# A table of 39 moves in the list scheduler of a hybrid encoder layer

## The chip, the core and the metric

The kernel runs on one core of a Trainium2 chip. The metric is the device time of one execution in microseconds. Five engines work at once, each strictly in the order of its own instruction queue: TensorE (PE, the matmuls), VectorE (DVE), ScalarE (ACT), GpSimd (POOL), and SyncE (SP), which does nothing here but issue DMAs. An instruction that has to wait for a semaphore holds up everything behind it on its engine, and a DMA that has to wait holds up every later DMA of the kernel, since all of them are issued from SP.

## The reference

One layer of a streaming encoder runs over 2048 prompt positions and, with its own state, over 32 positions of a second sequence (2080 columns together). All values are fp32. Cut to what matters:

```python
cs  = silu(c); mod = cs @ ada_w + ada_b                  # six vectors: shift, scale, gate, twice
h   = rmsnorm(x, g1) * (1 + sc1) + sh1
p   = h @ w_in                                           # 1024 -> 3080 columns
u, v = split(gelu(p[:, :1024])); v = rmsnorm(v)
a   = u * (W_s @ v + b_s)                                # spatial gating in chunks of 128 positions
q, k, v2 = split(silu(causal_conv(p[:, 1024:2560])))     # 4 heads of 128; q, k L2-normed
b   = gated_delta_rule(q, k, v2, beta, g, state)         # exact, evaluated in chunks (WY form)
b   = rmsnorm(b) * silu(z)
x   = x + gt1 * (concat(a, b) @ w_out)
h   = rmsnorm(x, g2) * (1 + sc2) + sh2
x   = x + gt2 * (relu(h @ w_up)**2 @ w_down)             # 1024 -> 4096 -> 1024
y   = rmsnorm(x, g3)
```

## The kernel before

**Tiling.** The activations lie transposed, channels on the 128 partitions, positions along the free dimension. The positions are worked in two halves (1024 and 1056 columns), and a half in groups of 512, or of 384, 384 and 288 columns. Every fp32 operand of a large product is split into a rounded part and a remainder (`BH` and `BL` for activations, `wh` and `wl` for weights), and a product is three matmuls, high by high, low by high and high by low, in `mm3`. A tile of the input projection is eight such triples (k = 0 to 7), accumulated in one PSUM bank. Three banks in a ring, called `g`, hold these tiles, so a tile can begin only when the tile three before it has been copied out by ACT. The feed-forward part runs over three blocks of positions with a Strassen form of the products; its PSUM tiles are called `f`.

**Stages.** First the adaLN modulation and the z columns, then for each half: the v columns and the spatial gating, the q, k, v columns with convolution (`qkv_tile`), for each head the local part of the delta rule (`delta_local`, PSUM bank `L`) and the inversion of its triangular blocks (`delta_inv`, bank `B`), the recurrence over the chunks (`delta_chain`, bank `C`), and the u columns. Then the output projection and the feed-forward part.

**Where the steps of the prediction stand.** `x_stats` runs in the middle of half 0 and prepares half 1. For each of the three groups of columns of half 1 it loads the eight 128-row pieces of x (`s<-xT`), squares them on ACT, adds the squares on POOL, turns the sums into 1/rms on PE (bank `M`, tile `M<-ones`) and writes normalised pieces back to DRAM (`h_d<-s`); the pieces pass through a ring of four half tiles named `E` (slots 21 and 22). `load_group` later loads these `h_d` pieces as the input of half 1, through the same ring. `qkv_tile` copies a PSUM tile out on ACT (`s<-g`), convolves on DVE (`L393`), applies SiLU on ACT, transposes 32 by 32 blocks on DVE (`L419`), writes q and k to DRAM (`kq_d<-s`) and the transposed blocks too (`kt_d<-s`). `delta_local` loads a pair of chunks of k and q back (`s<-kq_d`) and multiplies them on PE into bank `L`. Weights arrive by `wr<-w_b` and are split by ACT (`wh`) and DVE (`wl`).

**What sets the order.** The kernel records every operation as an `Op` with an engine, a class (`CHAIN`, `INV`, `LOCAL`, `EVAC`, `GEMM`), an estimated cost and its predecessors, 14596 operations in all. `Program.schedule` then replays them as a list scheduler: it keeps a modelled clock for each engine, lets an operation become ready when its predecessors' modelled ends and latencies have passed, and on each engine takes the ready operation with the smallest key. The key is the class, then a rank (for `EVAC` and `GEMM` the earliest matmul that depends on the operation, for the others its number), then the number. The order of the modelled starts is the order in which the instructions are emitted, and it fixes each engine's queue. Helpers record each operation, so that most instructions of a kind share one line: matmuls L436, transposes through PE L447, activations L373, DVE and POOL two-operand instructions L388 and L393, DMAs L426.

Of the kernel before, what the change touches and what calls it, by code (L numbers as in the profile page):

```python
# [45 lines left out]
PE, DVE, ACT, POOL, DMA, NONE = range(6)  # L46
# [15 lines left out]


CHAIN, INV, LOCAL, EVAC, GEMM, IDLE = range(6)
SLACK = 400
CALM = 1500
HOLD = {CHAIN: 300, INV: 300, LOCAL: 2000}
# [147 lines left out]
class Program:  # L215
# [19 lines left out]
    def op(self, eng, cost, fn, outs, ins, lat=0.0, table=None, after=()):  # L235
# [12 lines left out]
        o.hold = HOLD.get(self.prio, 0.0) if self.lax else 0.0  # L248
        o.slack = (SLACK if self.prio < GEMM else 0.0) + self.calm if eng == PE else 0.0
        o.npred, o.due = len(preds), self.due  # L250
# [5 lines left out]
    def schedule(self):  # L256

        ops = self.ops
        due = [i if o.eng == PE and o.prio == GEMM else len(ops) for i, o in enumerate(ops)]
        for i in reversed(range(len(ops))):  # L260
            due[i] = min([due[i]] + [due[j] for j in ops[i].succ] + ([] if ops[i].due is None else [ops[i].due]))
        turn = {LOCAL: EVAC, EVAC: LOCAL}
        key = [(o.prio if o.eng == PE else turn.get(o.prio, o.prio), due[i] if o.prio >= EVAC else i, i) for i, o in enumerate(ops)]
        free = [0.0] * 6
        port = [0.0] * 6
        wait = [[] for _ in range(6)]
        ready = [([], []) for _ in range(6)]
        table, large = None, True
        order, served, lands, flying = [], 0.0, [], []

        def release(i, t):
            o = ops[i]
            if o.eng == NONE:
                finish(i, t, t)
            else:
                heapq.heappush(wait[o.eng], (t, i))

        def finish(i, start, end):
            o = ops[i]
            o.start = start  # L280
            order.append((start, i))
            for j in o.succ:
                s = ops[j]
                s.ready = max(s.ready, end + o.lat + LATENCY.get((o.eng, s.eng), 0.0) + (s.slack if o.eng != PE else 0.0))
                s.npred -= 1
                if s.npred == 0:
                    release(j, s.ready)

        for i, o in enumerate(ops):
            if o.npred == 0 and o.start == 0.0 and o.eng != NONE:  # L290
                heapq.heappush(wait[o.eng], (0.0, i))
        for i, o in enumerate(ops):
            if o.npred == 0 and o.eng == NONE and not any(k == i for _, k in order[-1:]):
                finish(i, 0.0, 0.0)
                o.npred = -1

        other = {DVE: POOL, POOL: DVE}
        while True:
            best = None
            for e in range(5):  # L300
                shared = port[other[e]] - PORT if e in other else 0.0
                t = None
                if ready[e][0]:
                    t = free[e]
                elif ready[e][1]:
                    t = max(free[e], shared)
                if wait[e]:
                    at, i = wait[e][0]
                    at = max(free[e], at, shared if ops[i].port else 0.0)
                    t = at if t is None else min(t, at)  # L310
                if t is not None and (best is None or t < best[0]):
                    best = (t, e)
            if best is None:
                break
            t, e = best
            while wait[e] and wait[e][0][0] <= t:
                i = heapq.heappop(wait[e])[1]
                heapq.heappush(ready[e][ops[i].port if e != PE else ops[i].prio == GEMM], key[i])
            shared = port[other[e]] - PORT if e in other else 0.0
            tops = [q for q in (ready[e][0], ready[e][1] if shared <= t else None) if q]  # L320
            if not tops:
                continue
            top = min(tops, key=lambda q: q[0])
            if e == PE and large and len(tops) == 2 and all(t < ops[q[-1]].ready + ops[q[-1]].hold for q in tops[0]):
                top = tops[1]
            i = heapq.heappop(top)[-1]
            o = ops[i]
            end = t + o.cost
            if e == DMA and t < EARLY:
                t = max([t] + lands[-8:-7])  # L330
                flying = [q for q in flying if q[0] > t]
                over = sum(q[1] for q in flying) + o.runs - RUNS
                if over > 0:
                    for at, q in flying:
                        over -= q
                        if over <= 0:
                            break
                    heapq.heappush(wait[e], (at, i))
                    continue
                served = max(served, t + 2330) + o.size / (310 if t < 30000 else 350) + 50  # L340
                lands.append(served)
                flying.append((served, o.runs))
                end, o.lat = t + o.turn, served - t - o.turn + (0 if t < 30000 else 1000)
            if e == PE:
                large = o.prio == GEMM
            elif o.table and o.table != table:
                end += 1280
                table = o.table
            free[e] = end
            if o.port:  # L350
                port[e] = end
            finish(i, t, end)
        assert len(order) == len(ops), (len(order), len(ops))
        self.span = max(free)
        order.sort()
        return [ops[i] for _, i in order]
# [1747 lines left out]
```

## Time and profile before

| | |
|---|---|
| median of 3 runs | 2298.68 us (2298.04 to 2300.31) |
| the profiled execution's own time | 2300.34 us |
| its span, first to last instruction | 2298.2 us |
| PE busy | 2266.2 us (99%) |
| DVE, ACT, POOL busy | 1684.5, 1201.3, 554.0 us (73%, 52%, 24%) |
| DMA engines busy, mean | 73.1% of the span on the queue that SP issues to |

An engine's busy time is the union of its instructions; the ends of matmuls are modelled, since they are pipelined, so the distance between the starts of two matmuls says more than the length of one. PE is the bound where it is busy; where it is idle, the view of waits names what it waited for. The granted clock of TensorE is listed by stretch: 1.00 is full speed.

### The profile page before, as it was taken

To read this page: it belongs to the slowest core of one execution; us is meant where nothing else is said; L and a number is where in the kernel's file an instruction comes from. 1 tells how busy PE (TensorE), PEld (TensorE's weight loads), DVE (VectorE), ACT (ScalarE), POOL (GpSimd) and SP (SyncE) were. 2 spreads that over 40 slices of the span, in tenths; PEclk is the share of its full clock that TensorE was granted. 3 is DMA by queue.
4 is the path that set the end of the run, shared out by engine and by line. 5 is a ranking of instruction groups with operands and counts; after the bars stand their busy time and mean duration, and the time that the engine had idled before them with its cause. 6 is when DMAs were issued, how large, how long until landed. Compare 5 with 4: busy or idle time off the path is not lost.

```text
span 2298.2 us, 44733 instructions
## 1 busy us (share of the span) xinstructions
PE 2266.2 (99%) x15711; PEld 2155.6 (94%) x15711; DVE 1684.5 (73%) x3560; ACT 1201.3 (52%) x2556; POOL 554.0 (24%) x708
## 2 busy tenths in 40 slices
PE   9999899999999999999999999999999999999998
PEld 6787678999999889999999999999999999999998
DVE  7557676678763646599999989776668885666775
ACT  5555455665543534476555546653444564344344
POOL 1114431322313032444444424200001250000001
PEclk9999999999999999999999999999999999999999
DMA  9588877567666767987777777997668797666761
GB/s 331 166 277 262 225 206 227 164 183 188 155 174 195 250 198 238 298 281 259 256 253 264 251 271 249 342 312 234 213 214 267 253 309 231 218 219 216 248 220 55
DMA packets 426209, 538.49 MB, mean 234 GB/s; under 512 B 132976, under 2 KB 259324, under 8 KB 425984
## 3 DMA queue, kind: packets, MB, share of 16 engines
q1 hardware_dynamic: 425984, 535.63, 73.1%
q8 instruction: 124, 2.03, 0.4%
q14 instruction: 101, 0.83, 0.1%
HBM read 386.30 MB, written 149.18 MB: 233 GB/s over the span
## 4 chain that ended last, share of the span: by engine, by line
PE 85%; DMA 5%; DVE 4%; ACT 2%; SPq 2%; issue 1%; POOL 1%; POOLq 0%; DVEq 0%; ACTq 0%
PE f L436 53%; PE g L436 24%; PE C L436 3%; PE B L436 2%; SPq L426 2%; DVE s L393 2%; ACT s L373 1%; DVE s L388 1%; PE M L436 1%; PE L L436 1%; DMA s<-kq_d 1%; DMA s<-xT 1%; DVE wl L388 1%; DMA wr<-w_b 0%; DMA s<-x_d 0%
## 5 line engine op out<-in xcount | busy, mean ns | idle before, releaser
L373 ACT ACTIVATE s<-s 128x348 f32<-128x348 f32 (+13 forms) x1083 | 506.9, 492 | 327.0 <-DVE s L388 140.3
L436 PE MATMUL f<-s,wh 128*128 128x348 f32 (+1 forms) x2768 | 662.1, 322 | 0.4 <-DVE s L388 0.4
L436 PEld LDWEIGHTS f<-s,wh 128*128 128x128 f32 x2768 | 480.5, 188 | 2.0 <-DVE s L388 1.5
L388 DVE TENSOR_TENSOR s<-f,s 128x348 f32<-128x348 f32 (+1 forms) x696 | 348.1, 512 | 170.6 <-PE f L436 166.9
L436 PE MATMUL f<-s,wl 128*128 128x348 f32 (+1 forms) x1384 | 444.8, 321 | 0.1
L436 PE MATMUL g<-BH,wh 128*128 128x384 f32 (+2 forms) x1104 | 405.8, 368 | 0.9 <-ACT BH L373 0.8
L436 PE MATMUL g<-BL,wh 128*128 128x384 f32 (+2 forms) x1104 | 388.2, 352 | 0.5 <-DVE BL L393 0.5
L436 PE MATMUL g<-BH,wl 128*128 128x384 f32 (+2 forms) x1104 | 387.9, 351 | 0.4 <-DVE wl L388 0.4
L388 DVE TENSOR_TENSOR s<-s,s 128x348 fp32r<-128x348 f32 (+9 forms) x651 | 345.6, 560 | 45.1 <-ACT s L373 20.2
L436 PE MATMUL f<-BH,wh 128*128 128x348 f32 (+1 forms) x1024 | 330.0, 322 | 0.5 <-DVE s L388 0.5
L436 PE MATMUL f<-BL,wh 128*128 128x348 f32 (+1 forms) x1024 | 329.2, 321 | 0.0
L436 PE MATMUL f<-BH,wl 128*128 128x348 f32 (+1 forms) x1024 | 328.7, 321 | 0.0
L388 POOL TENSOR_TENSOR s<-s,s 128x512 f32<-128x512 f32 (+17 forms) x303 | 237.5, 788 | 369.2 <-ACT s L373 165.8
L373 ACT ACTIVATE wh<-s 128x512 fp32r<-128x512 f32 x282 | 176.4, 632 | 233.4 <-PE f L436 189.1
L436 PEld LDWEIGHTS f<-s,wl 128*128 128x128 f32 x1384 | 260.5, 188 | 0.4 <-DVE wl L388 0.4
L388 DVE TENSOR_TENSOR wl<-s,wh 128x512 fp32r<-128x512 f32 x282 | 217.4, 778 | 33.1 <-ACT wh L373 30.4
L436 PEld LDWEIGHTS g<-BH,wh 128*128 128x128 f32 x1104 | 208.5, 189 | 24.7 <-issue 5.6
L436 PEld LDWEIGHTS g<-BH,wl 128*128 128x128 f32 x1104 | 208.0, 188 | 20.2 <-DVE wl L388 0.8
L436 PEld LDWEIGHTS g<-BL,wh 128*128 128x128 f32 x1104 | 208.2, 189 | 17.1 <-DVE BL L393 0.8
L373 ACT ACTIVATE wh<-wr 128x512 fp32r<-128x512 f32 (+2 forms) x159 | 124.2, 782 | 134.7 <-PE f L436 60.8
L436 PEld LDWEIGHTS f<-BH,wh 128*128 128x128 f32 x1024 | 192.4, 188 | 1.1 <-DVE s L388 0.8
L436 PEld LDWEIGHTS f<-BH,wl 128*128 128x128 f32 x1024 | 193.0, 189 | 0.0
(129 smaller groups left out, 3133.1 us busy)
## 6 DMA issues: line engine op xcount, KB each, us to landing
s<-w_u SPq DMA_DIRECT2D x124, 256.0 KB, 3.6
s<-w_d SPq DMA_DIRECT2D x121, 256.0 KB, 3.2
wh<-su_d SPq DMA_DIRECT2D x114, 256.0 KB, 3.9
wl<-su_d SPq DMA_DIRECT2D x114, 256.0 KB, 4.1
wh<-sd_d SPq DMA_DIRECT2D x100, 256.0 KB, 3.2
wl<-sd_d SPq DMA_DIRECT2D x100, 256.0 KB, 3.7
wr<-w_b SPq DMA_DIRECT2D x36, 512.0 KB, 5.0
s<-adaw SPq DMA_DIRECT2D x32, 512.0 KB, 7.0
```

The costliest lines, as they stand in the source:

```text
L373: self.p.op(ACT, c, lambda: nc.scalar.activation(out=R(out), in_=R(in_), func=func, **{k: R(v) for k, v in kw.items()}), [out, accum], [in ...
L388: self.p.op(eng, c, lambda: e.tensor_tensor(out=R(out), in0=R(a), in1=R(b), op=op), [out], [a, b])
L393: self.p.op(DVE, c, lambda: nc.vector.scalar_tensor_tensor(out=R(out), in0=R(a), scalar=R(s), in1=R(b), op0=op0, op1=op1), [out], [a, s, b])
L426: self.p.op(DMA, max(500, x), lambda: nc.sync.dma_start(out=R(out), in_=R(in_)), [out], [in_], lat=LAND + b / RATE - max(500, x))
L436: nc.tensor.matmul(R(out), R(l), R(r), **kw)
```

## The change

The scheduler takes a table `MOVES` of 39 rows `(first, n, shift, ns)`. A row applies to those of the n operations from number `first` on that have the engine and the class of operation `first`. `shift` is added to their rank in the key; `ns` is added to the time at which they become ready in the scheduler's modelled clock (nothing in the emitted program waits for it). No operation is added, removed or altered, and the tiles stay in the same places; only the order of the instructions on the engines changes, and with it the points at which one engine waits for another. 30 rows have a delay, 9 a shift.

```diff
+MOVES = [
+    (1137, 6, 0, 785), (4449, 24, 0, 1), (35, 1, -6283, 0), (6079, 1, 0, 13035), (195, 40, 0, 156), (1608, 40, 0, 3551),
...
+]
...
-        key = [(o.prio if o.eng == PE else turn.get(o.prio, o.prio), due[i] if o.prio >= EVAC else i, i) for i, o in enumerate(ops)]
+        rank = [due[i] if o.prio >= EVAC else i for i, o in enumerate(ops)]
+        late = [0.0] * len(ops)
+        for first, n, shift, ns in MOVES:
+            for j in range(first, min(first + n, len(ops))):
+                if (ops[j].eng, ops[j].prio) == (ops[first].eng, ops[first].prio):
+                    rank[j] += shift
+                    late[j] += ns
+        key = [(o.prio if o.eng == PE else turn.get(o.prio, o.prio), rank[i], i) for i, o in enumerate(ops)]
...
                 if s.npred == 0:
+                    s.ready += late[j]
                     release(j, s.ready)
```

The orders differ in the two halves of the mixer (the first 900 us of the profile before) and in patches of the first block of the feed-forward part up to about 1495 us. Behind that no instruction changes its place. The source has 18 more lines, so L436 before is L454 after, L426 is L444, L373 is L391. The numbers in the tiles' names count emitted tiles and differ for the same tile; g_3019 before and g_2964 after are the same tile of the input projection, and so are g_2890 and g_2866, and g_2742 and g_2755.

PE in half 0, where head 2's `delta_local` begins: bank `L` multiplies the first loaded pair of chunks, and `M<-ones` sums the squares of the third group of `x_stats`. Before:

```order
L436 MATMUL g_2890<-BH_78,wh 128x512
L436 MATMUL g_2890<-BL_86,wh 128x512
L436 MATMUL g_2890<-BH_78,wl 128x512
L436 MATMUL L_2894<-s_474 128x256 x2
L436 MATMUL M_2643<-ones,s_478 128x1 x3
L436 MATMUL g_3019<-BH_71,wh 128x512
L436 MATMUL g_3019<-BL_79,wh 128x512
```

After (the rows of g_2964 that stand ahead of these are its first three triples, BH_71 to BH_73, behind the last one of g_2866):

```order
L454 MATMUL g_2964<-BH_74,wh 128x512
L454 MATMUL g_2964<-BL_82,wh 128x512
L454 MATMUL g_2964<-BH_74,wl 128x512
L454 MATMUL L_2858<-s_474 128x256 x2
L454 MATMUL g_2964<-BH_75,wh 128x512
L454 MATMUL g_2964<-BL_83,wh 128x512
L454 MATMUL g_2964<-BH_75,wl 128x512
```

Four triples of the next tile now stand ahead of the `L` pair, and the `M` sums, which stood right behind it, stand twenty triples later.

SP's queue ahead of the load that this `L` pair multiplies (`s_474<-kq_d_99`, two DMAs). Before:

```order
L426 DMA nd_d_0_163<-s_491 16x8x16 x8
L426 DMA s_489<-xT 128x288 x2
L426 DMA kt_d_0_105<-s_475 32x32x32
L426 DMA s_488<-xT 128x288
L426 DMA kq_d_99<-s_487 128x512
L426 DMA s_488<-xT 128x288
L426 DMA s_473<-nd_d_0_163 128x256
L426 DMA kq_d_99<-s_487 128x512
L426 DMA wr_96<-w_b 128x1024
L426 DMA pk_d_3_126<-s_473 128x256
L426 DMA s_489<-xT 128x288
L426 DMA s_474<-kq_d_99 128x2x256 x2
```

After:

```order
L444 DMA pk_d_3_126<-s_473 128x256
L444 DMA nd_d_0_163<-s_491 16x8x16 x8
L444 DMA h_d_159<-s_489 128x384
L444 DMA h_d_160<-s_489 128x384
L444 DMA h_d_161<-s_488 128x384
L444 DMA h_d_162<-s_488 128x384
L444 DMA kq_d_99<-s_487 128x512 x2
L444 DMA s_473<-nd_d_0_163 128x256
L444 DMA s_489<-xT 128x288 x2
L444 DMA s_488<-xT 128x288 x2
L444 DMA s_474<-kq_d_99 128x2x256 x2
L444 DMA wr_96<-w_b 128x1024
```

Of all DMAs ahead of the load, from the start of the kernel, six are behind it now: five loads of x for the third group and one of weights; none has come ahead of it. The last `kt_d` write, which stood between the loads of x, stands ahead of the eight `nd_d` writes now, and the four `h_d` writes of the second group have come down to this place.

ACT at the same place: copies of PSUM tiles (`s_485<-g_...`), squares of the third group (128x288), SiLU and squares of the convolved tiles (`s_487`, `s_486`). Before:

```order
L373 ACTIVATE s_478<-s_489 128x288
L373 ACTIVATE s_489<-s_489 128x288
L373 ACTIVATE s_488<-s_488 128x288 x2
L373 ACTIVATE wh<-wr_96 128x1024
L373 ACTIVATE s_489<-s_489 128x288 x2
L373 ACTIVATE s_488<-s_488 128x288
L373 ACTIVATE s_486<-s_475 128x512
L373 ACTIVATE s_488<-s_488 128x288
L373 ACTIVATE s_486<-s_475 128x512
L373 ACTIVATE s_486<-s_485,s_484 128x512 x2
L373 ACTIVATE wh<-wr_96 128x1024
L373 ACTIVATE s_485<-g_2742 128x512
```

After:

```order
L391 ACTIVATE s_486<-s_475 128x512 x2
L391 ACTIVATE s_486<-s_485,s_484 128x512 x2
L391 ACTIVATE wh<-wr_96 128x1024
L391 ACTIVATE s_485<-g_2755 128x512
L391 ACTIVATE s_485<-g_2848 128x512
L391 ACTIVATE s_487<-s_486 128x512 x2
L391 ACTIVATE s_478<-s_489 128x288
L391 ACTIVATE s_489<-s_489 128x288
```

The eight squares of the third group stood ahead of the copy of the tile (g_2742, now g_2755); they all stand behind it and behind the next tile's copy now.

6 rows, old and new, of the table MOVES are left out of this document.

## The prediction

> **What bounds the kernel now.** I read the totals first, then the windows by stage, then the view of PE's waits, and last the timelines around the longest one.
>
> ```profile
> span 2298.2 us, 44733 instructions
> ```
>
> The windows give, for each stretch, its length and the busy time of PE, PEld, DVE, ACT and POOL, then the granted clock of TensorE:
>
> ```profile
> core 0: us, PE busy (x) PEld busy (x) DVE busy (x) ACT busy (x) POOL busy (x), PEclk, DMA share, GB/s
> 0.00:200.00 200.00, 195.20 (x1308) 151.97 (x1308) 126.02 (x287) 110.57 (x199) 41.86 (x62) 1.00 0.77 258
> 200.00:277.64 77.64, 77.57 (x346) 63.09 (x344) 55.77 (x103) 39.38 (x76) 31.65 (x39) 1.00 0.86 235
> 277.64:281.90 4.26, 0.00 (x1) 0.00 (x0) 2.01 (x3) 2.13 (x5) 2.47 (x6) 0.99 0.89 290
> 281.90:286.10 4.20, 0.00 (x0) 0.02 (x1) 4.09 (x7) 2.29 (x3) 3.81 (x7) 0.50 0.94 324
> 286.10:292.10 6.00, 5.99 (x17) 5.05 (x18) 3.51 (x6) 2.13 (x5) 3.40 (x8) 0.50 0.38 104
> 292.10:370.00 77.90, 77.90 (x774) 63.38 (x774) 55.25 (x108) 41.27 (x75) 21.86 (x40) 1.00 0.78 216
> 370.00:780.00 410.00, 402.30 (x3891) 388.22 (x3890) 281.53 (x827) 233.67 (x581) 103.50 (x275) 1.00 0.66 185
> 780.00:1500.00 720.00, 718.10 (x4403) 695.66 (x4402) 591.73 (x1080) 408.70 (x863) 280.12 (x213) 1.00 0.78 264
> 1500.00:2277.00 777.00, 777.00 (x4908) 776.90 (x4907) 551.57 (x1121) 353.03 (x736) 61.25 (x58) 1.00 0.72 232
> 2277.00:2298.20 21.20, 12.13 (x77) 11.28 (x75) 13.04 (x25) 8.10 (x16) 4.11 (x4) 0.78 0.38 134
> ```
>
> PE is the bound everywhere, and a change of order adds and removes no matmul. What it can win is PE's idle time, length minus busy time of a row: 4.8 us in the first 200, 8.5 between 277.64 and 286.10, nothing up to 370, 7.7 up to 780, 1.9 up to 1500, nothing up to 2277, 9.1 in the tail. To this comes a clock of 0.50 from 281.9 on, the only dip before the tail. From about 1495 on no instruction changes its place, so the tail's 9.1 us stay. About 23 us stand in stretches that the table touches, and half of that is one event.
>
> **The event.** The waits of PE (engine and line, who ended the wait, us in total, times, longest):
>
> ```profile
> PE L L436 <- DMA s<-kq_d: 9.6, 2, 8.5
> PE C L436 <- DVE s L393: 1.5, 3, 0.7
> PE B L436 <- DVE s L419: 1.0, 1, 1.0
> PE C L436 <- DMA s<-ada: 0.2, 1, 0.2
> ```
>
> One wait of 8.5 us stands above a field of waits of about 1. PE's timeline around it (start, length, what, idle time before it and its releaser):
>
> ```profile
> 277.24 0.40 PE L436 MATMUL g<-BH,wl 128*128 128x512 f32 x1
> 286.11 2.04 PE L436 MATMUL L<-s 128*128 128x256 f32 x4 [8.47 <-DMA s<-kq_d]
> 290.09 0.63 PE L436 MATMUL g<-BH,wl 128*128 128x512 f32 x1
> 291.37 0.63 PE L436 MATMUL g<-BH,wl 128*128 128x512 f32 x1
> 292.40 0.39 PE L436 MATMUL g<-BH,wl 128*128 128x512 f32 x1
> 293.10 0.39 PE L436 MATMUL g<-BH,wl 128*128 128x512 f32 x1
> ```
>
> A triple takes 292.40 to 293.10, 0.70 us, at full clock and 290.09 to 291.37, 1.28 us, at half clock. Two things come late at once. First, the operand: SP issues the `kq_d` load only at 280.04, after a file of other DMAs, and it lands 5.93 us later (SP's timeline, then the row of the chain of waits):
>
> ```profile
> 269.66 4.52 SPq L426 DMA_DIRECT2D nd_d<-s  x8
> 274.28 0.85 SPq L426 DMA_DIRECT2D s<-xT  x2
> 275.18 0.42 SPq L426 DMA_DIRECT2D kt_d<-s  x1
> 275.70 0.51 SPq L426 DMA_DIRECT2D s<-xT  x1
> 276.99 0.38 SPq L426 DMA_DIRECT2D s<-xT  x1
> 278.49 0.38 SPq L426 DMA_DIRECT2D wr<-w_b  x1
> 279.50 0.44 SPq L426 DMA_DIRECT2D s<-xT  x1
> 280.04 1.20 SPq L426 DMA_DIRECT2D s<-kq_d  x2
> ...
> 280.04 5.93 DMA s<-kq_d
> ```
>
> Second, the bank: the tile that would have filled the hole needs the bank of the tile three before it, and ACT copies that one out only at 286.24. ACT is held by squares that wait for loads of x, DVE by a transpose that waits for the `kt_d` write and then by ACT:
>
> ```profile
> 277.92 1.25 DVE L419 STREAM_TRANSPOSE s<-s 128x1024 f32<-128x1024 f32 x1 [1.23 <-DMA kt_d<-s]
> 278.82 1.06 ACT L373 ACTIVATE s<-s 128x288 f32<-128x288 f32 x2 [1.29 <-DMA s<-xT]
> 281.82 0.69 DVE L1218 TENSOR_REDUCE s<-s 128x16 f32<-128x512 f32 x1 [1.22 <-ACT s L373]
> 286.24 0.60 ACT L373 ACTIVATE s<-g 128x512 f32<-128x512 f32 x1 [0.70 <-DVE s L393]
> ```
>
> **The change at this place.** The orders show three moves.
>
> *The operand.* Six DMAs leave the file ahead of the load: the rows at 274.28 (two), 275.70, 276.99, 278.49 and 279.50, together 2.56 us of issue, 2.9 with the gaps of about 0.05 us between issues. The load goes out at about 280.04 - 2.9 = 277.1 and lands at 283.1. The `kt_d` write goes out ahead of the `nd_d` writes and the first x loads, 4.52 + 0.85 us and more earlier.
>
> *The cover.* Four triples, 4 x 0.70 = 2.8 us, now stand ahead of the `L` pair, so PE reaches it at 277.64 + 2.8 = 280.4. From the operand alone 283.1 - 280.4 = 2.7 us of the wait remain.
>
> *The bank.* These triples need the copy that ended at 286.84. With the `kt_d` write out at about 269 and landed after as long as before (275.18 to 277.92, 2.7 us), the transpose is no longer held by it; it is by the weight split ahead of it, for which ACT waits less now. I put it some 4 us earlier. From there to the copy it was 286.24 - 277.92 = 8.3 us, in which the squares hold ACT for 1.29 us of waiting and 1.06 of work, and DVE waits 1.22 us for ACT; take 3 off. The copy then starts at about 279. The triples wait 1 to 2 us for it, and what they wait is taken off the wait for the load. So between 0 (the file of SP also runs ahead, as its loads of x no longer wait for a free `E` half) and 5.7 us (the load goes out no earlier: 286.1 - 280.4) remain. I take 2, since the counted issues give 2.7 and the waits in front of them can only shrink. Gain 8.5 - 2 = 6.5.
>
> *The clock.* It fell to half 4.26 us after PE went idle, and PE worked 6.0 us at 0.50, which would have taken 3.0 at full clock. After a wait of 2 us I expect no dip: the other waits of 1.0 us above left the clock at 1.00. Gain 3.0. The Trainium skill, "TensorE: Matmul & The Clock Gate", section "What's actually happening", says that the gate watches a free-running window of about 3.4 us and halves the clock after an idle one. The trace agrees as far as it goes (a drop 4.26 us after the start of the idle time). The formula in that page's section "Terms" (the Trainium skill), throttled time by (1 - K/N), would make it 10.2 x 0.5 = 5.1 us, but PE was idle in 4.2 us of the throttled stretch, so the row decides: 3.0. The rule speaks against the change in one way: a remaining wait beyond about 3.4 us keeps the dip.
>
> **The rest of the mixers and the first block.** 7.7 us of idle time up to 780 and 1.9 up to 1500 are made of waits of 1.3 us or less for DVE, ACT and DMAs. The moves reorder nearly every queue there, so any of these waits can go and others come. Bounds: all go, -9.6; as many again come, +9.6. I followed two of them through the orders. Around 1361, eighteen triples more stand ahead of the one that waited. Around 692, five DMAs leave SP's file ahead of the second late `kq_d` load, but nineteen groups of matmuls leave PE's queue ahead of its product, so that one is open. I take -2: somewhat more eased than added, since the moves are many and a tighter queue has its own surprises.
>
> **The start.** One load of `ada` weights moves from third to first on SP, past two loads that it delays by one issue, 0.4 us by the rows above; PE waited 0.2 us for `ada`. Between -0.2 and +0.4; I take 0, since PE is then held by the weights behind, whose place is unchanged.
>
> **Late next.** The third statistics group: its sums on PE stand 24 triples (16.7 us of work) further down, less the 6.5 us won ahead of them, so some 10 us later, and half 1's inputs with them. Rows that bound this, from the views of the tiles `h_d` and `BL`:
>
> ```profile
> L426 SPq DMA_DIRECT2D h_d<-s x8: 320/338/411, 298.1 to 315.6; - x8
> L426 SPq DMA_DIRECT2D s<-h_d x24: 319/380/1430, 312.5 to 383.6; - x24
> L436 PE MATMUL g<-wh,BL x92: 277/282/288, 363.2 to 419.9; 128*128 128x260 f32 x92
> ```
>
> The last write went out at 315.6, the first product of half 1 ran at 363.2: 47 us of cover for a delay of 10. I cost it at nothing; without cover it would be 10.
>
> **Sum.** -6.5 - 3.0 - 2 + 0 = -11.5 us, on a span of 2298.2: 2286.7. The execution took 2300.34 in all, 2.1 more than its span, which the change does not touch; the median of the runs is 2298.68, so I forecast 2298.68 - 11.5 = 2287 us. With 5.7 to 0 left of the wait and the small waits from +2 to -6 the case itself spans 2281 to 2294.
>
> **Rivals.**
> 1. *The wait hardly shrinks.* If SP's file is held by what it waits for and not by its length, the load goes out at 280.04 as before and 5.7 us remain; that is over the 4.26 us after which the clock fell, so the dip stays. Gain 2.8: 2296. For it: the eight `nd_d` issues take 4.52 us, where eight of 0.43 with gaps of 0.05 take 3.8, so SP waited 0.7 us in there. Against it: from 274.28 to 280.04 issues follow each other with no wait.
> 2. *Every small wait goes too.* -8.5 - 3.0 - 9.6 = -21: 2278. For it: the table is spread over the whole mixer. Against: 39 rows cannot be aimed at a score of waits of 1 us that each depend on when a DMA lands.
> 3. *New waits eat the gain.* The place is mended, and as much idle time appears where the queues are reordered: 2298. For it: the field of small waits shows that the order is tight; against: it would need more new idle time than that whole stretch has now.
> 4. *Slower: half 1 starts late.* The postponed statistics share the `E` ring with `load_group`, so loads of half 1 queue behind them on SP, and all later DMAs behind those. It decides once the delay of 10 us grows beyond the 47 us of cover, through SP being blocked by a load that waits for an `h_d` write. PE would then idle by the whole 16.7 us of moved work and run 6 us at half clock: -11.5 + 16.7 + 3.0: 2307. Against it: the cover.
>
> **How the numbers follow.** A measurement of this kernel tells 0.2%, 4.6 us, from no change. Forecast 0.62, rivals 0.10, 0.13, 0.07, 0.08. Faster: forecast and rival 2, and a little of rival 1: 0.77. Same: the rest of rival 1 and rival 3: 0.15. Slower: 0.08. The range leaves out the slower rival and the outer half of rival 2: 2279 to 2297.
>
> **What would show it.** The profile after should have the `L` wait behind g_2964's fourth triple at 0 to 3 us, no clock of 0.50 before the tail, the copies of the two tiles ahead of the squares, 402 of 410 or more busy between 370 and 780, and the stretch of 777 us behind the reordered part as long as now. A `kq_d` load that goes out no earlier, or a wait of PE for `BH` or `BL` around 350 to 370, would make it wrong.

## The result and the profile after

| | before | changed |
|---|---|---|
| median of the runs, us | 2298.9 (2298.0 to 2300.3, 4 runs) | 2286.8 (2286.0 to 2287.9, 4 runs) |
| profiled execution, us | 2300.34, span 2298.2 | 2286.02, span 2284.2 |
| PE busy / idle in the span, us | 2266.2 / 32.0 | 2260.6 / 23.6 |

The ratio is 0.9947, 95% interval 0.993 to 0.9964: 12.1 us faster, where 11.5 were forecast. Between the two profiled spans the difference is 14.0 us, 8.4 of it idle time of PE and 5.6 busy time; the profiled execution of before (2300.34) lies above its four runs, and that of the changed kernel is the fastest of its four, so this pair shows more than the medians.

The windows of the changed kernel, in the columns of the prediction (length, then busy PE, PEld, DVE, ACT, POOL, then the granted clock):

```profile
span 2284.2 us, 44702 instructions
...
277.64:292.10 14.46, 12.51 (x53) 9.95 (x54) 10.12 (x12) 9.98 (x21) 13.55 (x27) 1.00 0.90 244
292.10:370.00 77.90, 77.18 (x803) 64.08 (x802) 53.38 (x109) 41.82 (x75) 23.58 (x35) 1.00 0.78 228
370.00:780.00 410.00, 406.04 (x3891) 390.92 (x3890) 285.80 (x828) 235.64 (x587) 110.51 (x276) 1.00 0.68 193
780.00:1500.00 720.00, 718.48 (x4435) 700.22 (x4434) 594.08 (x1099) 414.01 (x879) 283.19 (x214) 1.00 0.79 265
```

At the place near 278 us the one wait of 8.5 us and the clock of 0.50 are gone; between 370 and 780 us 4.0 us of idle time are left of 7.7. PE's timeline, the rows of the changed kernel in which it waited for data between 276 and 330 us, and then SP and ACT there (line numbers are 18 higher than before):

```profile
277.70 0.50 PE L454 MATMUL g<-BH,wh 128*128 128x512 f32 x1 [1.14 <-ACT s L391]
282.65 1.10 PE L454 MATMUL L<-s 128*128 128x256 f32 x4 [1.90 <-DMA s<-kq_d]
304.66 0.54 PE L465 MATMUL M<-ident,rcol 128*128 128x128 f32 x3 [0.72 <-POOL rcol L406]
```

```profile
275.81 2.03 SPq L444 DMA_DIRECT2D s<-xT  x4
277.93 1.18 SPq L444 DMA_DIRECT2D s<-kq_d  x2
```

```profile
277.05 1.26 ACT L391 ACTIVATE s<-g 128x512 f32<-128x512 f32 x2 [2.06 <-DVE s L411]
```

The load goes out at 277.93 instead of 280.04, the copies of two tiles start at 277.05, where before the first of them started at 286.24, and four triples stand ahead of `L`. What is left of the wait is 1.14 us for the bank and 1.90 for the load, in two pieces. The stretch behind the reordered part is as long as it was within 1 us: from its first matmul to the last transposes through PE 1498.14 to 2289.86 us before, 1483.09 to 2275.84 after.

So far everything reads as forecast. The experiments show that the forecast's account of the 12 us was nevertheless too simple.

### The profile page after: what moved, and what is told of

Same layout as the page of the kernel before. It is cut to its first block, busy times and chain, and to the rows that moved or that the text cites. A ratio compares the mean times of both kernels' runs of the same rounds, so it can differ in the third digit from the quotient of the medians.

```text
span 2284.2 us, 44702 instructions
## 1 busy us (share of the span) xinstructions
PE 2260.6 (99%) x15711; PEld 2153.7 (94%) x15711; DVE 1681.1 (74%) x3560; ACT 1212.4 (53%) x2566; POOL 565.9 (25%) x708
## 4 chain that ended last, share of the span: by engine, by line
PE 85%; DMA 5%; DVE 4%; ACT 2%; issue 1%; SPq 1%; POOL 1%; POOLq 0%; DVEq 0%; ACTq 0%
PE f L454 53%; PE g L454 24%; PE C L454 3%; PE B L454 2%; ACT s L391 1%; PE L L454 1%; DVE s L411 1%; SPq L444 1%; PE M L454 1%; DVE s L406 1%; DMA wr<-w_b 1%; DVE wl L406 1%; POOL s L406 1%; DMA s<-xT 1%; DMA s<-th_d 0%
## 5 line engine op out<-in xcount | busy, mean ns | idle before, releaser
L391 ACT ACTIVATE s<-s 128x348 fp32r<-128x348 f32 (+11 forms) x1083 | 506.8, 493 | 317.2 <-DVE s L406 131.9
L454 PE MATMUL f<-s,wh 128*128 128x348 f32 (+1 forms) x2768 | 661.6, 322 | 1.5 <-DVE s L406 0.8
L454 PEld LDWEIGHTS f<-s,wh 128*128 128x128 f32 x2768 | 480.5, 188 | 2.6 <-DVE s L406 1.3
L454 PE MATMUL f<-s,wl 128*128 128x348 f32 (+1 forms) x1384 | 444.7, 321 | 0.0
L454 PE MATMUL g<-BH,wh 128*128 128x384 f32 (+2 forms) x1104 | 404.8, 367 | 2.7 <-issue 1.2
L454 PE MATMUL g<-BL,wh 128*128 128x384 f32 (+2 forms) x1104 | 387.8, 351 | 0.5 <-DVE BL L411 0.5
L454 PE MATMUL g<-BH,wl 128*128 128x384 f32 (+2 forms) x1104 | 387.4, 351 | 0.0
L406 DVE TENSOR_TENSOR s<-s,s 128x348 fp32r<-128x348 f32 (+8 forms) x651 | 347.8, 564 | 46.2 <-ACT s L391 19.2
L406 POOL TENSOR_TENSOR s<-s,s 128x512 f32<-128x512 f32 (+18 forms) x303 | 248.3, 825 | 347.5 <-ACT s L391 156.6
L454 PE MATMUL f<-BH,wh 128*128 128x348 f32 (+1 forms) x1024 | 330.2, 322 | 0.7 <-ACT wh L391 0.5
L454 PE MATMUL f<-BL,wh 128*128 128x348 f32 (+1 forms) x1024 | 329.0, 321 | 0.0
L454 PE MATMUL f<-BH,wl 128*128 128x348 f32 (+1 forms) x1024 | 328.8, 321 | 0.0
L391 ACT ACTIVATE wh<-s 128x512 fp32r<-128x512 f32 x282 | 176.4, 632 | 238.5 <-PE f L454 205.8
L454 PEld LDWEIGHTS f<-s,wl 128*128 128x128 f32 x1384 | 260.5, 188 | 0.0
L406 DVE TENSOR_TENSOR wl<-s,wh 128x512 fp32r<-128x512 f32 x282 | 211.9, 760 | 34.7 <-ACT wh L391 34.7
L454 PEld LDWEIGHTS g<-BH,wh 128*128 128x128 f32 x1104 | 207.8, 188 | 25.7 <-issue 5.2
L454 PEld LDWEIGHTS g<-BH,wl 128*128 128x128 f32 x1104 | 207.7, 188 | 19.4
L454 PEld LDWEIGHTS g<-BL,wh 128*128 128x128 f32 x1104 | 207.8, 188 | 18.4 <-issue 1.3
L391 ACT ACTIVATE wh<-wr 128x512 fp32r<-128x512 f32 (+2 forms) x159 | 124.2, 782 | 141.0 <-PE f L454 63.9
L454 PEld LDWEIGHTS f<-BH,wh 128*128 128x128 f32 x1024 | 192.4, 188 | 1.5 <-ACT wh L391 0.8
L454 PEld LDWEIGHTS f<-BH,wl 128*128 128x128 f32 x1024 | 193.0, 188 | 0.0
```

The lines of the kernel that those rows point to most:

```text
L391: self.p.op(ACT, c, lambda: nc.scalar.activation(out=R(out), in_=R(in_), func=func, **{k: R(v) for k, v in kw.items()}), [out, accum], [in ...
L406: self.p.op(eng, c, lambda: e.tensor_tensor(out=R(out), in0=R(a), in1=R(b), op=op), [out], [a, b])
L454: nc.tensor.matmul(R(out), R(l), R(r), **kw)
```

## The experiments

The theory at the outset: the place at 278 us is worth 8 to 9 us (5.4 us of wait, 3.0 of clock), the field of small waits the rest, and the two add up. The rival: the gain belongs to the order as a whole, and a stretch of it alone keeps little. All ratios are to the kernel before on the same chip, with their 95% intervals.

| kernel | median, us | before there | ratio |
|---|---|---|---|
| early order only, seam at 290 us | 2298.3 | 2298.1 | 0.9999 (0.9990 to 1.0007) |
| late order only | 2292.3 | 2298.1 | 0.9977 (0.9967 to 0.9987) |
| 36 products ahead of `L` | 2300.7 | 2298.1 | 1.0009 (0.9999 to 1.0019) |
| triples ahead of `L`, PE alone | 2300.4 | 2298.1 | 1.0009 (1.0000 to 1.0018) |
| before, again | 2298.8 | 2298.9 | 1.0000 (0.9992 to 1.0009) |
| changed, again | 2282.9 | 2298.9 | 0.9938 (0.9926 to 0.9950) |
| early order, seam at 360 us | 2293.9 | 2298.9 | 0.9981 (0.9971 to 0.9991) |
| 24 products ahead of `L` | 2298.6 | 2298.9 | 1.0004 (0.9994 to 1.0015) |
| the nine early rows of the table | 2297.0 | 2298.2 | 0.9992 (0.9982 to 1.0002) |
| the other thirty rows | 2305.3 | 2298.2 | 1.0028 (1.0015 to 1.0042) |
| the table less one row | 2323.0 | 2298.2 | 1.0098 (1.0084 to 1.0112) |
| changed, three moves by hand | 2285.6 | 2298.2 | 0.9938 (0.9926 to 0.9951) |

### The order cut in two

Two kernels plan both orders and join them at one point, the seam: the operations that one order starts before the seam, then all others in the sequence of the other order. No table row, delay or price differs from the two kernels; only which stretch follows which. (The number in the condition is the scheduler's own clock; on the chip the seam lies at about 290 us.)

```diff
+        table = self.plan(MOVES)
...
+        plain = self.plan([])
+        first = [i for t, i in table if t <= 280000]
+        seen = set(first)
+        return [ops[i] for i in first + [i for _, i in plain if i not in seen]]
```

> The order of the changed kernel up to about 290 us of the span, and from there on the remaining operations in the order of before. My theory: the gain sits at the one place at 278 us, where 8.5 us of wait and 3.0 us of half clock became 1.14 + 1.90 us of wait, so this kernel keeps 8 to 9 us of the 12: about 2290 us. Rival, that the 39 moves gain a little everywhere: the first eighth of the span keeps less than 5 us, 2294 us or above.

Measured: no gain (between 2.3 us faster and 1.6 slower). PE's timeline shows the place mended (1.54 us of wait at `L`), and then this, just behind the seam:

```profile
281.31 1.10 PE L465 MATMUL L<-s 128*128 128x256 f32 x4 [1.54 <-DVE s L1247]
291.87 1.44 PE L465 MATMUL M<-ones,s 128*128 128x1 f32 x6 [2.48 <-POOL s L417]
294.50 0.90 PE L476 MATMUL M<-ident,rcol 128*128 128x128 f32 x3 [1.20 <-POOL rcol L417]
```

These are the postponed statistics. The early order sends their loads behind the `kq_d` load; the late order of before asks for their sums `M` as soon as it did. PE waits 2.48 us for the sums and 1.20 for `rcol`, the 1/rms values made of them, both from POOL, and the clock falls to half for 6.8 us. By this profile mending the place pays only if `M` is postponed on PE too.

The reverse: before's order up to the seam, the changed one behind it (`plain` and `table` change places in the code; the condition stays at 280000).

> The reverse: the order of before up to about 298 us, the order of the changed kernel from there on. My theory: the hole of 8.5 us and the half clock stay at 277.64 us, and only the small waits go (3.7 us between 370 and 780 us, next to nothing elsewhere): 3 to 4 us gained, about 2295 us. Rival, gains everywhere: 7 us or more, 2292 us or below.

Measured: 5.3 us (ratio by 2298; 3.0 to 7.6), more than the 3 to 4 us of the theory, though the interval reaches down to them. Its profiled execution was its fastest, 2.6 us under its median. The wait for the operand is there, with the clock at half for 10.2 us, and the stretch behind it is what changed: 1.7 us of idle time between 350 and 800 us, where the profile shown of before has 7.7. PE's timeline and a window of this kernel, then the same window of before:

```profile
284.80 2.04 PE L465 MATMUL L<-s 128*128 128x256 f32 x4 [6.81 <-DMA s<-kq_d]
```

```profile
350.00:800.00 450.00, 448.35 (x4190) 428.99 (x4190) 314.40 (x905) 256.23 (x635) 120.47 (x282) 1.00 0.69 201
```

```profile
350.00:800.00 450.00, 442.30 (x4110) 422.15 (x4109) 302.63 (x878) 250.73 (x617) 110.61 (x278) 1.00 0.67 191
```

### Both kernels once more

The executions of before spread over 11 us on the chip of the first set, so both were taken again, with profiles of their own.

> The kernel before, unchanged, with a profile of its own beside the ones that it is compared with: the earlier runs of it spread over 11 us here (2291.9 to 2303.2), where the three of the first set lay within 2.3 us. Both theories: no change, 2296 to 2300 us. What is read is its wait ahead of the L pair: if it is about 7 us instead of 8.5, the 36 products of the no-dip kernel (8.0 us) overran the operand and hid 1 us or more of what the clock gave back.

> The changed kernel, unchanged, beside the other three: 11 to 13 us under before, about 2286 us, by every theory; it is the measure for the two halves.

The medians stand (2298.8; 2282.9, even 16 us under). But the place is not the same in this execution of before. Its wait ahead of `L`, and its windows:

```profile
284.28 2.05 PE L436 MATMUL L<-s 128*128 128x256 f32 x4 [5.34 <-DMA s<-kq_d]
```

```profile
250.00:350.00 100.00, 94.66 (x806) 75.66 (x805) 67.41 (x111) 51.13 (x91) 33.06 (x65) 0.97 0.82 227
283.90:290.70 6.80, 6.42 (x18) 5.42 (x19) 4.26 (x7) 2.56 (x5) 4.43 (x10) 0.50 0.47 136
350.00:800.00 450.00, 441.81 (x4105) 422.49 (x4104) 302.06 (x877) 250.59 (x618) 110.15 (x278) 1.00 0.66 191
```

The same order left PE without work for 8.47 us there in one execution, 5.34 in another, and for 6.81 and 6.23 in two kernels of this study that share it up to this point (the late order only, and the other thirty rows, where two neighbouring DVE instructions at 247 us change places). The prediction took the largest of these for the size of the wait. A second load of the same kind was later in this execution than in the first, 2.3 us at 673 us against 1.1 (before's waits of PE between 350 and 800 us):

```profile
PE L L436 <- DMA s<-kq_d: 2.3, 1, 2.3
PE C L436 <- DVE s L393: 1.5, 2, 0.9
```

The second profile of the changed kernel, the same windows, has 2.9 and 1.0 us of idle time, and no wait for `kq_d` but the one at 281 us:

```profile
250.00:350.00 100.00, 97.10 (x828) 77.28 (x827) 69.97 (x111) 55.37 (x96) 35.56 (x65) 1.00 0.81 227
350.00:800.00 450.00, 449.00 (x4168) 430.53 (x4167) 311.37 (x900) 255.95 (x636) 121.34 (x283) 1.00 0.69 200
```

```profile
281.10 1.10 PE L454 MATMUL L<-s 128*128 128x256 f32 x4 [1.40 <-DMA s<-kq_d]
303.18 0.54 PE L465 MATMUL M<-ident,rcol 128*128 128x128 f32 x3 [0.80 <-POOL rcol L406]
321.99 0.30 PE L454 MATMUL B<-s,s 32*32 32x16 f32 x13 [0.69 <-issue]
```

By this pair the place gives 2.4 us of idle time and 3.2 of clock (half of 6.42 us busy at 0.50), the stretch behind it 7.2.

### The seam moved behind the statistics

The early-only kernel with `t <= 350000`, so that `M` and the transposes behind it keep their later places.

> As the early-only kernel, but with the seam at about 360 us of the span instead of 290, so that the sums M of the postponed statistics and the transposes behind them keep their later places too. Theory A (the place is worth its 8 to 9 us as long as the postponed statistics stay postponed on TensorE as well; the early-only kernel lost it where M came due again at 289 us): 8 to 9 us under before, about 2290 us. Theory B (TensorE does not set the end of this stage; what it gains at 278 us it waits for again before 780 us in any order but that of the whole table): 0 to 3 us under before, 2295 us or above.

Measured: 4.4 us (2.1 to 6.7), between the theories. PE arrives at 350 us with the place's gain (idle time of 2.2 us between 250 and 350), and gives part of it back at the new seam. Its longest waits between 355 and 385 us, where neither profile of before has any:

```profile
PE C L465 <- DVE s L422: 1.8, 3, 0.7
PE C L465 <- ACT s L402: 0.9, 2, 0.5
```

So the first kernel lost the gain at its seam, as supposed; the size of the place cannot be read from a kernel with a seam, wherever it lies.

### The clock dip by itself

Before, with products of the matrix of ones put ahead of the `L` pair, into the bank that the pair overwrites. Nothing else moves.

```diff
+        n = len(self.p.ops)
+
         def fn():
+            for _ in range(36 if n == 1966 else 0):
+                nc.tensor.matmul(R(calls[0][0][:, :P]), R(self.ones), R(self.ones), start=True, stop=True)
             for out, l, r, kw in calls:
```

> Before, with 36 products of the 128x128 matrix of ones (about 0.22 us each, 8.0 us in all) put on TensorE just ahead of the L pair, into the bank that the pair then overwrites; the load of the operand stays as late as it was. My theory: L still starts at 286.1 us, but the clock stays at 1.00, and the 3.0 us that the rows behind the wait took longer at half clock come back: about 2296 us. By the formula of the page of the Trainium skill on the clock gate it would be 5.1 us: about 2294 us. Rival, that what was slow behind the wait would have waited anyhow: no change, 2299 us.

> The no-dip kernel with 24 products instead of 36 (5.3 us instead of 8.0), so that they end before the operand lands even if it lands 1.7 us sooner than in the first profile. If the half clock costs its 3.0 us of time: about 2295 us, 3 us under before. If what TensorE gets back is waited for again further on: 2297 to 2300 us, no change, with the clock at 1.00 all the same.

With 36 the products filled the whole wait; as it is between 5.3 and 8.5 us long, they may have run over the operand. With 24 they did not in the profiled execution. PE's timeline (the 24 products leave 48 records), and the window of the place:

```profile
278.38 5.52 PE L438 MATMUL L<-ones 128*128 128x128 f32 x48
285.33 1.13 PE L440 MATMUL L<-s 128*128 128x256 f32 x4 [1.44 <-DMA s<-kq_d]
```

```profile
277.64:292.10 14.46, 13.02 (x87) 11.57 (x86) 10.65 (x15) 8.43 (x14) 10.97 (x24) 1.00 0.78 228
```

The clock stays at 1.00 in this execution, and the `L` pair takes 1.13 us instead of 2.04. Yet the kernel is not faster: between 1.4 us faster and 3.4 slower with 24, between 0.2 faster and 4.4 slower with 36. A gain of 3.0 us lies outside both. An estimate by the formula of the Trainium skill, "TensorE: Matmul & The Clock Gate", section "Terms", would have been 5.1 us (10.2 us at half clock, times one half); these runs bear out neither that nor the row's 3.0 as a saving of the whole kernel.

They do not refute 3.0 us as the price of the half clock either. The 36 products can cost what they save, where they overrun the operand. Of the eleven executions with 24, five have a mean granted clock of 0.995 or 0.996, as low as those of before (0.994 to 0.996), so the clock fell in these as well, at the place or elsewhere. And the profiled one (0.998) kept what it won. The transposes of `rcol` behind the place, in the two profiles of before and then here:

```profile
295.42 0.49 PE L447 MATMUL M<-ident,rcol 128*128 128x128 f32 x3
293.80 0.49 PE L447 MATMUL M<-ident,rcol 128*128 128x128 f32 x3
291.84 0.49 PE L451 MATMUL M<-ident,rcol 128*128 128x128 f32 x3
```

It leads by 3.6 and 2.0 us there, and by 4.8 and 3.4 at the end of its span of 2293.4 us. But it was the fastest but one of its kernel, and one profile does not hold an average. What the clock is worth by itself stays open.

### The triples by themselves

```diff
...
+        at = out.index(1966)
+        ahead = [2018, 2057, 2266, 2267, 2268, 2269, 2270]
+        out = out[:at] + ahead + [i for i in out[at:] if i not in ahead]
```

1966 is the `L` pair, 2267 to 2270 are the four triples, the others what they need; on each engine but PE the sequence stays.

> Before, with one thing moved: the four triples of the next GEMM tile stand ahead of the L pair on TensorE, every other engine as it was. Theory of one late operand (the load of the pair): the triples fill 2.8 us of the wait, 2296 us. My theory of two late things at once: the triples' bank is emptied by a copy that ScalarE ends at about 286.8 us only, behind the squares, so that TensorE waits at the triples instead of at the pair, and nothing is gained: 2298 to 2300 us, clock dip and all.

Measured: not faster (ratio 1.0000 to 1.0018). PE waits at the triples instead, for the copy of the bank, and the copy waits for DVE:

```profile
284.54 0.79 PE L440 MATMUL g<-BH,wh 128*128 128x512 f32 x1 [7.24 <-ACT s L377]
```

```profile
283.88 0.60 ACT L377 ACTIVATE s<-g 128x512 f32<-128x512 f32 x1 [1.29 <-DVE s L397]
```

Here the theory of two late things at once holds: with work at hand but no bank for it, nothing is won.

### The table cut in two, and one row less

Without a seam: the table itself is cut, and the scheduler plans on from whatever order it has. Nine rows name operations of the first 300 us; they alone make the changed order up to there. The other thirty alone leave before's order up to there.

```diff
-MOVES = [
-    (1137, 6, 0, 785), (4449, 24, 0, 1), (35, 1, -6283, 0), ...
...
+MOVES = [(1137, 6, 0, 785), (35, 1, -6283, 0), (195, 40, 0, 156), (960, 12, 0, 1046), (1057, 40, 0, 3709), (908, 150, 0, 583), (304, 12, -5, 0), (965, 12, 1, 0), (1366, 150, 0, 234)]
```

> The table cut to the nine of its 39 rows that name operations of the first 300 us; the scheduler itself goes on from there, so no seam. Theory A (the place at 278 us is worth 8 to 9 us, and the early-only and the early-to-360 kernels lost 9 and 6 of it at their seams): 8 to 9 us under before, about 2290 us. Theory B (whatever is gained at 278 us is waited for again by 780 us): 0 to 3 us under before.

> The other thirty rows without the nine: the wait at 278 us stays. Theory A (rows are worth what the stretch is worth that they order): 5 to 6 us under before, as the rest-only kernel, about 2293 us. Theory C (each row is right only behind the order that the rows before it make; in another order its delay falls on another moment): 0 to 3 us under before, or slower.

> The table without one of its rows, the one that shifts 12 operations by 5 ranks, (304, 12, -5, 0). If the rows act each for itself, one of 39 is worth about a third of a microsecond: no difference from the changed kernel, 12 to 16 us under before. Theory C: the order behind 250 us is another one, in which a GEMM tile's operands stand late; a wait of 5 us or more comes back near 278 us, and the kernel is at most 5 us under before, perhaps slower than it.

The nine rows: 1.8 us (4.1 faster to 0.5 slower). The place is mended (4.2 us of idle time from 250 to 350, no half clock there), the next stretch is even better than before, and a stretch that the nine rows do not name has become worse: 5.5 us of idle time from 800 to 1500, where before has 1.9 and 1.3. The windows, and PE's waits from 800 to 1500 us:

```profile
250.00:350.00 100.00, 95.85 (x812) 76.33 (x811) 69.21 (x107) 51.81 (x93) 35.84 (x66) 1.00 0.81 220
350.00:800.00 450.00, 444.25 (x4149) 424.81 (x4148) 310.24 (x905) 255.40 (x635) 113.66 (x281) 1.00 0.69 198
800.00:1500.00 700.00, 694.53 (x4262) 676.08 (x4261) 582.45 (x1044) 394.82 (x830) 279.18 (x210) 1.00 0.77 260
```

```profile
PE f L446 <- DVE s L403: 2.0, 1, 2.0
PE f L446 <- DVE s L398: 1.7, 3, 0.9
```

The thirty rows: 6.4 us slower (3.4 to 9.7), with the wait at 278 us in place and new ones where neither kernel has any, 5.9 us between 912 and 946 us:

```profile
PE g L446 <- DVE s L403: 4.0, 3, 2.0
PE g L446 <- ACT BH L383: 1.9, 1, 1.9
```

Apart the two parts of the table give 1.8 and -6.4 us, together 12 to 14. They do not add up. One row less, five ranks of twelve operations, is the plainest case: 22.5 us slower than before, with a bank 16 us late at the very place that the whole table mends, and PE busy for 9.2 us of 25.3 there at a mean clock of 0.66 (timeline, then window):

```profile
287.79 0.79 PE L446 MATMUL g<-BH,wh 128*128 128x512 f32 x1 [16.07 <-ACT s L383]
```

```profile
268.00:293.30 25.30, 9.23 (x29) 7.01 (x29) 10.93 (x14) 12.01 (x27) 13.04 (x27) 0.66 0.78 201
```

### Three moves by hand

The changed order, with the two `kq_d` writes ahead of the `h_d` writes, its two loads ahead of the four loads of x, and the `rcol` transposes four triples later:

```diff
+        for moved, behind in (([1919, 1937], 983), ([1964, 1972], 996)):
+            out = [i for i in out if i not in moved]
+            at = out.index(behind)
+            out = out[:at] + moved + out[at:]
...
+        for i in (1024, 1025, 1026):
+            place[i] = place[2663] + 0.001 * (i - 1000)
...
```

> The changed kernel with three things moved in its order by hand: the two writes of kq_d of this head ahead of the four writes of h_d, the two loads of it ahead of the four xT loads behind them (so that the load ahead of the L pair is issued at about 275.8 instead of 277.9 us), and the three transposes of rcol behind four more triples. By the waits of the two profiles of the changed kernel (1.4 to 1.9 us for the load, 0.7 to 0.8 us for rcol): 2 to 2.7 us under the changed kernel, if nothing comes in their place. Rival: these waits are made good by others behind them, no difference from the changed kernel.

Measured: a ratio of 0.9938, where the changed kernel had 0.9947 and 0.9938. With intervals of about 3 us each way the times cannot tell a gain of 2 to 2.7 us from none, so the profile has to. The waits for the load and for `rcol` are gone: the load goes out at 275.06, and `L` runs at 279.48 without a wait. Four others stand in their place, 2.74 us together, against 2.89 in the second profile of the changed kernel up to 330 us:

```profile
294.89 0.83 PE L466 MATMUL M<-ones,s 128*128 128x1 f32 x6 [0.46 <-POOL s L418]
311.37 0.50 PE L466 MATMUL g<-BH,wl 128*128 128x512 f32 x1 [0.83 <-DVE wl L418]
320.40 0.91 PE L466 MATMUL B<-s,s 32*32 32x16 f32 x64 [0.56 <-DVE s L432]
323.80 0.73 PE L466 MATMUL B<-s,s 32*32 32x16 f32 x64 [0.89 <-DVE s L418]
```

In this profile PE came earlier and met POOL and DVE where they were. The version that would beat the changed kernel was not found.

## Why the prediction was right, and where not

The time was right: 2287 forecast, 2286.8 measured. That it came within 0.2 us is luck, since an oversized and an undersized term cancel, and the second measurement of the changed kernel, 16 us under before, was missed by 4.5. By its steps:

- *The operand.* Out at 277.1, landed at 283.1: it was 277.93 and 282.6. Held by four loads of x at 275.81, but 4.7 us under way instead of 5.9.
- *The cover and the bank.* The copy at about 279, 1 to 2 us of waiting for it: it was 277.05 and 1.14. That triples alone win nothing is shown by the kernel that moved them alone.
- *The residue of 2 us.* 3.04 in one profile, 1.40 in the other.
- *The gain of 6.5 us at the wait.* 8.47 - 3.04 = 5.4 by the first pair of profiles, 5.34 - 1.40 = 3.9 by the second. Oversized, because it was made against one execution, and this wait happened to be the longest of those seen.
- *The clock, 3.0 us.* No half clock before the tail, as forecast. The executions outside the profiles agree: their mean granted clock is 0.997 to 0.999, where before has 0.994 to 0.996. As a term of the sum it is not borne out: taking the dip out by itself made the kernel no faster in the median, though one profile kept the gain.
- *The small waits, 2 us.* Undersized: 3.7 us between 370 and 780 by the first pair, 7.2 between 350 and 800 by the second, 5.3 in time by the late order alone. The question left open in that step, whether the second late `kq_d` load would still be waited for, is answered: neither profile of the changed kernel has that wait.
- *The start, 0.* The waits for `ada` were 0.2 and 1.7 us in the two profiles of before, 1.2 and 1.0 in those of the changed kernel: no effect of the move can be told from this.
- *The statistics, 0.* No wait for `BH` or `BL` near 360 us, so the fourth rival is out; but a wait of 0.7 to 0.8 us for `rcol` near 304 us is new, and the early-only kernel shows what they cost when `M` is not postponed with them.

Of the 5.6 us of PE's busy time that the first pair differs by, 3.0 are the rows at half clock. The other 2.6 stand in no term, and what they are is not shown; they belong to the order behind 300 us, since the late-only kernel, which has the half clock at its place still, was busy for 2262.5 us against 2266.2 of before.

The upper end of the case, 2294, also counts the clock as won while 5.7 us of the wait remain; by the prediction's own first rival such a wait keeps the dip.

The step that does not hold is the sum itself. It took the wait at 278 us as a gain that stands by itself, with the rest as a small correction. The third rival, that new waits eat the gain, is what the nine rows alone do; the second, that every small wait goes, is close to what the changed kernel did in its second profile (1.0 us left between 350 and 800). The 12 us belong to one whole order. What can be said of its parts is this: with the changed order behind it, the mended place is worth the difference of two ratios, 0.9977 and 0.9938 to 0.9947, that is 7 to 9 us, give or take 4 (what the seam of the late-only kernel costs is in it); with another order behind it between nothing and 4.4.

Open are three things: what the clock is worth as time; which of the moves took the small waits out of the stretch behind 350 us; and whether the waits behind 800 us of the nine rows come from PE's earlier arrival or only from another plan there. The kernel by hand shows waits that follow an earlier arrival within 40 us, not over 500.

## What to carry to other kernels

A list scheduler's order is one piece: price a change of it by the waits of the whole new order, not by the wait that it mends, since a row less can cost nearly twice what the table wins, and the larger part of it alone half as much. Where PE is 99% busy and other engines run close behind it, as here, a wait removed by hand can come back at the next thing that is not ready (here within 40 us, in one profile); so ask whether everything behind can come earlier too. And before a single wait carries a forecast, look at it in a second execution: this one measured 8.5 us and 5.3.

## What the runs showed of the hardware

The clock falls after shorter waits than I had thought. Its records come in steps of 3.41 us: every stretch at half clock inside the kernels is 3.41, 6.83, 10.24 or 17.07 us long. Three windows with a wait in them, one of before's second profile and two of the nine rows, each with the window behind it:

```profile
672.99:676.40 3.41, 1.07 (x7) 0.87 (x5) 0.70 (x2) 0.63 (x2) 0.00 (x0) 1.00 0.85 258
676.40:679.81 3.41, 3.41 (x14) 3.40 (x13) 2.17 (x4) 1.47 (x3) 0.00 (x0) 0.50 0.34 95
```

```profile
717.99:721.40 3.41, 1.73 (x71) 1.38 (x70) 1.90 (x5) 0.00 (x0) 3.10 (x9) 1.00 0.68 195
721.40:724.81 3.41, 3.41 (x73) 2.93 (x72) 1.12 (x5) 1.95 (x7) 2.71 (x10) 0.50 0.85 284
281.08:284.49 3.41, 1.54 (x8) 1.31 (x8) 2.80 (x4) 2.57 (x5) 3.25 (x8) 1.00 0.83 226
284.49:287.90 3.41, 3.41 (x16) 2.75 (x15) 3.19 (x6) 1.06 (x1) 3.02 (x6) 1.00 1.01 282
```

A window with 1.07 us of PE work, and one with 1.73, were each followed by a window at half clock; one with 1.54 was not. The waits in them were 2.34, 1.68 and 1.87 us. The Trainium skill, "TensorE: Matmul & The Clock Gate", section "What's actually happening", has the window of about 3.4 us, and the steps agree with it; that it takes an idle window to fall, the rows do not bear out: about half a window can be enough. Busy time by itself does not draw the line, as 1.73 fell and 1.54 did not; the 1.73 were partly products of 32x32 tiles, but whether that is the reason was not tried.
